# An encoder block on one core: the front is loaded in smaller pieces, and work is moved ahead of the plan

## The chip, the cores and the metric

The kernel runs on one core of a Trainium2 chip. The metric is the device time of one execution in microseconds, from the runs of one program; lower is better. TensorE (PE in the profile) does the matrix products, ScalarE (ACT) and VectorE (DVE) evaluate and split, GpSimd (POOL) takes a share of the elementwise work, and SyncE (SP) issues nearly all transfers.

## What is computed

One block of a hybrid encoder in float32 on 512 tokens of width 1024, with 16 learned meta tokens in front (528 columns). Two mixers work on the same normalized input: windowed attention with 16 query heads on 4 key heads, in a band of three 128-token blocks with the meta keys and a sink, and differential attention with 8 heads over all keys. Sigmoid gates merge them, and a gated feed-forward layer follows.

```python
u = rms_norm(h, pre_mix_gain[l])
proj = u @ w_in[l]
qa, ka, va, qb, kb, vb, g = jnp.split(proj, SPLITS, axis=-1)
...
o_swa = windowed_gqa_sink_attention(qa, ka, va, attn_sink[l], pos, is_real)
o_diff = differential_attention(qb, kb, vb, lam, lambda_init, subln_gain[l], is_key)
gates = jax.nn.sigmoid(g + b_gate[l])
merged = g_swa * (o_swa @ w_branch_swa[l]) + g_diff * (o_diff @ w_branch_diff[l])
h = h + rms_norm(merged @ w_out[l], post_mix_gain[l])
u = rms_norm(h, pre_ffn_gain[l])
f = (jax.nn.silu(gate_up[..., :D_FF]) * gate_up[..., D_FF:]) @ w_ffn_out[l]
```

## The kernel before

**Precision.** A float32 operand is split into a high part, rounded by a copy on ACT, and a low part, the difference, taken on DVE or POOL. Each product is made of three matmuls (`mm3`): high by high (L286), high weight by low input (L287), low weight by high input (L288). The third can't start before the whole low weight tile (`wl`) is written.

**Weights.** One tile of weights is 128 x 1024, 512 KB. SP loads it into one of three raw buffers (`wr`), ACT casts it (`wh`), DVE or POOL subtracts (`wl`). A raw buffer is free when the subtraction has read it, so a load in SP's queue can wait for POOL or DVE, and what stands behind it in the queue waits too. There are three slots each for `wh` and `wl`.

**The front** is written out by hand, L359 to L484, in the order in which each engine shall run it:

- 60 products of a zeroed tile (`warm`, L363) on PE.
- The input, transposed, comes in eight pieces `xr` of 264 KB (L375), and each is scaled by the gain on ACT (`xh`, L379), with its low part on DVE (`xl`, L380). Between them stand the weights of the two halves of the keys, in two pieces of 256 KB each (`w_half`, L388). All these transfers are issued by SP.
- The keys' products go through the eight input pieces k, twelve 264-column matmuls each, into `kA` and `kB`. Then the first value tile (`pV`, 48 matmuls, into the PSUM tiles `tr`).
- The sums of squares of the rows (`ss`, L440 and L442) give the row scale `rst`. Its columns are spread out on DVE (`rb`), transposed on PE (L454, L457), and copied by ACT to `rbc`. The keys' products are copied to `kraw`. `rbc` scales values (`VT`, L567), rotary factors (`rot`, L630) and all later evictions.

**The plan.** From there to the end of the differential attention (L621 to L1023), a table of tasks with costs, priorities and due times is scheduled by `Plan.run` while the program is built: each engine takes the task that is ready first and due first, at the plan's own costs. The result is a fixed order for each engine. Score products, transposes and products with the values have the first priority; the 512-column products of later weight tiles (queries, gates) are filler, put in wherever nothing more urgent is ready by the plan's clock. `held` takes over tiles made in the front.

The plan of before starts with the second value tile (`w3`) as a task. `v_swa` scales, transposes and splits the values. `rope_t` rotates keys and queries: products with `rot` on DVE (`ta`, `tb`, L533), a sum on POOL (L545), high part on ACT (L541) and low part on DVE (L537) into the one buffer `hl`. From there SP moves rows to the key tiles `KK` and query tiles `Q` (L555). `hl` holds the keys first; the queries' rotation writes it when the keys' moves have read it. `s_swa(u)` makes the scores of unit u of 16 (L692), `t_swa(u)` transposes them (L741) and multiplies by the values (L748). `gate(j)` is one gate tile of 24 matmuls of 512 columns. A table gives the unit after which each gate becomes available.

## Time and profile before

| | |
|---|---|
| time before, median of 3 runs | 983.13 us (981.66 to 983.18) |
| the profiled execution's own time | 984.33 us |
| its span, first to last instruction | 982.5 us |
| PE busy | 960.4 us, 98% |
| DVE, ACT, POOL busy | 572.5, 446.1, 287.8 us |

The span begins with the first instruction, and all times below count from there. The profiled execution is 1.83 us longer than its span, and 1.20 us above the median. The front fills about the first 26 us; the keys' and first queries' part of the plan lasts to 74 us, where the first scores stand; the windowed attention lasts to about 222 us. Behind 500 us PE has next to no idle time until its work ends.

### The profile page before, as it was taken

What the parts mean: (1) busy time and instruction counts of PE and PEld (TensorE: products, weight loads), DVE (VectorE), ACT (ScalarE), POOL (GpSimd) and SP (SyncE); (2) the same over time, 40 slices, a digit from 0 to 9 for tenths busy, and PEclk for the clock granted to TensorE, in tenths of its full rate; (3) what the DMA queues carried; (4) which work ended last, traced back from release to release, by engine and by line L of the source; (5) the groups of instructions that cost most, each with busy time, mean ns of one, the idle gap of its engine ahead of it and who ended that gap; (6) DMA issues with size and microseconds to landing.
All of it is one profiled execution on the core that took longest, in us unless ns stands there. A gap on an engine that the chain in (4) does not pass through costs nothing.

```text
span 982.5 us, 14257 instructions
## 1 busy us (share of the span) xinstructions
PE 960.4 (98%) x5307; PEld 825.3 (84%) x5307; DVE 572.5 (58%) x1061; ACT 446.1 (45%) x828; POOL 287.8 (29%) x262
## 2 busy tenths in 40 slices
PE   9899999999999999999999999999999999999997
PEld 9777777889798999999888888998888888888885
DVE  5836897899564758877765837843334333313224
ACT  6326676675634446667646434632222223222221
POOL 0543454453132423234203312653434300000000
PEclk9999999999999999999999999999999999999999
DMA  9482122251425144433531742343232323234122
GB/s 339 136 217 67 63 76 65 75 130 44 131 86 146 50 118 122 130 95 100 153 108 45 241 142 65 130 150 106 88 107 86 107 88 105 88 105 132 60 65 86
DMA packets 37141, 109.34 MB, mean 111 GB/s; under 512 B 6080, under 2 KB 6592, under 8 KB 37072
## 3 DMA queue, kind: packets, MB, share of 16 engines
q1 hardware_dynamic: 37072, 108.43, 36.4%
q8 instruction: 42, 0.69, 0.3%
q14 instruction: 27, 0.22, 0.1%
HBM read 87.04 MB, written 2.10 MB: 91 GB/s over the span
## 4 chain that ended last, share of the span: by engine, by line
PE 84%; DVE 8%; DMA 3%; issue 2%; SPq 2%; ACT 2%; DVEq 0%; POOL 0%; ACTq 0%
PE pr L287 18%; PE pr L288 18%; PE pr L286 18%; PE Sd L840 3%; PE Sw L692 2%; PE wk L288 2%; PE wk L286 2%; PE wk L287 2%; PE tr L288 2%; PE tr L287 2%; PE tr L286 2%; PE tr L880 2%; PE O L748 1%; PE Od L893 1%; PE acc L288 1%
## 5 line engine op out<-in xcount | busy, mean ns | idle before, releaser
L252 POOL TENSOR_TENSOR wl<-wr,wh 128x768 fp32r<-128x768 f32 (+1 forms) x76 | 170.8, 2248 | 235.0 <-ACT wh L271 155.7
L286 PE MATMUL pr<-xh,wh 128*128 128x264 f32 (+1 forms) x616 | 200.3, 325 | 0.0
L287 PE MATMUL pr<-xl,wh 128*128 128x264 f32 (+1 forms) x616 | 196.5, 319 | 0.4 <-DVE xl L380 0.4
L288 PE MATMUL pr<-xh,wl 128*128 128x264 f32 (+1 forms) x616 | 196.5, 319 | 0.3 <-POOL wl L252 0.3
L271 ACT CAST wh<-wr 128x1024 fp32r<-128x1024 f32 x78 | 81.9, 1052 | 216.5 <-PE pr L287 84.4
L252 DVE TENSOR_TENSOR wl<-wr,wh 128x1024 fp32r<-128x1024 f32 (+2 forms) x110 | 107.7, 980 | 121.0 <-ACT wh L271 109.1
L288 PEld LDWEIGHTS pr<-xh,wl 128*128 128x128 f32 x616 | 116.0, 188 | 9.0 <-POOL wl L252 0.5
L287 PEld LDWEIGHTS pr<-xl,wh 128*128 128x128 f32 x616 | 116.3, 189 | 8.1 <-DVE xl L380 0.6
L286 PEld LDWEIGHTS pr<-xh,wh 128*128 128x128 f32 x616 | 116.3, 189 | 7.4
L287 PE MATMUL pr<-ul,wh 128*128 128x512 f32 (+1 forms) x304 | 110.7, 364 | 0.3 <-DVE ul L252 0.3
L286 PE MATMUL pr<-uh,wh 128*128 128x512 f32 (+1 forms) x304 | 110.9, 365 | 0.0
L288 PE MATMUL pr<-uh,wl 128*128 128x512 f32 (+1 forms) x304 | 110.6, 364 | 0.0
L508 ACT CAST wh<-wr 128x1024 fp32r<-128x1024 f32 x56 | 58.6, 1049 | 43.7 <-PE pr L287 32.8
L287 PEld LDWEIGHTS pr<-ul,wh 128*128 128x128 f32 x304 | 57.4, 189 | 9.7 <-DVE ul L252 0.5
L288 PEld LDWEIGHTS pr<-uh,wl 128*128 128x128 f32 x304 | 57.3, 189 | 9.1
L286 PEld LDWEIGHTS pr<-uh,wh 128*128 128x128 f32 x304 | 57.3, 189 | 9.0
L545 POOL TENSOR_TENSOR ta<-ta,tb 128x528 f32<-128x528 f32 (+1 forms) x26 | 36.4, 1401 | 79.1 <-DVE tb L533 53.1
L845 DVE TENSOR_REDUCE nm<-Sd 128x1 f32<-128x528 f32 x64 | 45.2, 705 | 21.8 <-PE Sd L840 20.9
L308 POOL TENSOR_TENSOR r3y<-r3v,mhalf 128x1 f32<-128x1 f32 x4 | 2.2, 552 | 186.9 <-DVE r3v L307 186.9
L706 POOL TENSOR_SCALAR p<-p,rc 128x272 f32<-128x272 f32 (+1 forms) x64 | 37.1, 594 | 57.1 <-DVE rc L704 57.1
L848 ACT ACTIVATE pp<-Sd,nm 128x528 f32<-128x528 f32 x40 | 28.0, 700 | 39.3 <-DVE pa L861 22.6
L699 ACT ACTIVATE p<-p,nm 128x273 f32<-128x273 f32 (+1 forms) x64 | 36.7, 574 | 18.7 <-DVE nm L695 18.3
(377 smaller groups left out, 2000.4 us busy)
## 6 DMA issues: line engine op xcount, KB each, us to landing
wr<-in_w_in_dram SPq DMA_DIRECT2D x50, 512.0 KB, 4.2
wr<-in_w_fi_dram SPq DMA_DIRECT2D x50, 512.0 KB, 3.5
wr<-in_w_fo_dram SPq DMA_DIRECT2D x22, 512.0 KB, 3.5
Kd<-hl SPq DMA_DIRECT2D x32, 132.0 KB, 2.4
Kd<-Kd SPq DMA_DIRECT2D x16, 264.0 KB, 4.0
Q<-hl SPq DMA_DIRECT2D x64, 64.0 KB, 2.0
Qd<-hl SPq DMA_DIRECT2D x64, 64.0 KB, 2.5
wr<-in_w_bs_dram SPq DMA_DIRECT2D x8, 512.0 KB, 4.0
```

The source lines that it names most:

```text
L252: (eng or dve).tensor_tensor(out=lo, in0=src, in1=hi.bitcast(F32), op=ALU.subtract)
L271: act.copy(out=wh, in_=raw)
L286: pe.matmul(out=ps, lhsT=ah, rhs=bh, start=first, stop=False)
L287: pe.matmul(out=ps, lhsT=ah, rhs=bl, start=False, stop=False)
L288: pe.matmul(out=ps, lhsT=al, rhs=bh, start=False, stop=last)
L508: T("ACT", 1.05, lambda: act.copy(out=wh.t, in_=wr.t), r=[wr], w=[wh], prio=pr_)
L545: T("POOL", 0.05 + 1.3 * m, lambda: pool.tensor_tensor(out=ta.t[:, :, 0:n], in0=ta.t[:, :, 0:n], in1=tb.t[:, :, 0:n], op=ALU.add), r=[tb], ...
L699: T("ACT", 0.4 + 0.42 * c, lambda hh=hh: act.activation(out=pt.t[:, hh, 0:nk + 1], in_=pt.t[:, hh, 0:nk + 1], func=AF.Exp, scale=-1.0, bia ...
L706: T("POOL", 0.2 + 0.43 * c, lambda z=z: pool.tensor_scalar(out=pt.t[:, z, 0:nk], in0=pt.t[:, z, 0:nk], scalar1=rc.t[:, z:z + 1], scalar2=1 ...
L840: pe.matmul(out=S.t[:, s, 0:HALF], lhsT=Q[c].t[:, i * P:(i + 1) * P], rhs=K[c].t[:, x, s * HALF:(s + 1) * HALF], start=(x == 0), stop=(x = ...
L845: T("DVE", 0.71, lambda S=S, c=c, one=one: dve.tensor_reduce(out=nm.t[:, c, one], in_=S.t[:, :, 0:HALF], axis=AX.XY, op=ALU.min), r=[S], w ...
L848: T("ACT", 0.9, lambda S=S, c=c, one=one, p=p: act.activation(out=p().rearrange("p (a b) -> p a b", a=2), in_=S.t[:, :, 0:HALF], func=AF.E ...
```

## The change

- The keys' weights come in three pieces, k 0, k 1 to 3 and k 4 to 7 (64, 192 and 256 KB). ACT issues the first piece of both halves and the second piece of the first half; SP issues the rest. The split of a piece is called apart from its load.
- 40 zero products instead of 60.
- The second value tile is multiplied in the front, half of it ahead of the transposes of the row scale and half behind. `kraw` is copied ahead of the sums of squares.
- The first query tile's weights are loaded and split in the front, the low part on POOL.
- The plan starts with engines free at other times (`free`), slots and SP at earlier ones, and two tables are changed: gates 2 to 5 become available after units 1, 8, 11, 14 instead of 0, 1, 2, 8, and the first two counts of `b1` are swapped.

```diff
@@ Plan @@
-        self.slots = {t: [0.0] * n for t, n in tags.items()}
+        self.slots = {t: [-9.0] * n for t, n in tags.items()}
...
-        free = dict.fromkeys(("PE", "ACT", "DVE", "POOL", "SP"), 0.0)
-        port = 0.0
+        free = dict(PE=0.0, ACT=-1.2, DVE=-1.2, POOL=-0.5, SP=-3.0)
+        port = -9.0
...
-                    t = 0.0
+                    t = -9.0
@@ front @@
-    for _ in range(60):
+    for _ in range(40):
         pe.matmul(out=wps[:, 0:P], lhsT=warm, rhs=warm, start=True, stop=True)
...
-    def w_half(w, n, h):
-        if h == 0:
+    def w_part(w, n, k0, k1, eng):
+        if k0 == 0:
             w.extend([...])
-        ks = slice(h * KT // 2, (h + 1) * KT // 2)
-        sp.dma_start(out=w[0][:, ks], in_=I["w_in"][n].rearrange("p (k c) -> p k c", k=KT)[:, ks])
-        split(w[1][:, ks], w[2][:, ks], w[0][:, ks])
+        ks = slice(k0, k1)
+        eng.dma_start(out=w[0][:, ks], in_=I["w_in"][n].rearrange("p (k c) -> p k c", k=KT)[:, ks])
+        return lambda: split(w[1][:, ks], w[2][:, ks], w[0][:, ks])
...
     x_load(0)
-    w_half(wA, 0, 0)
+    sa = w_part(wA, 0, 0, 1, act)
+    sb_ = w_part(wB, 1, 0, 1, act)
+    x_load(1)
+    sa1 = w_part(wA, 0, 1, 4, act)
+    sa()
     x_split(0)
-    w_half(wB, 1, 0)
-    for k in range(1, KT):
+    sb1 = w_part(wB, 1, 1, 4, sp)
+    sb_()
+    x_load(2)
+    x_split(1)
+    sa1()
+    sb1()
+    for k in range(3, KT):
         x_load(k)
-        x_split(k)
-        if k == 2:
-            w_half(wA, 0, 1)
-            w_half(wB, 1, 1)
+        x_split(k - 1)
+        if k == 3:
+            sa2, sb2 = (w_part(w, n, 4, KT, sp) for n, w in enumerate((wA, wB)))
+        if k == 4:
+            sa2()
+            sb2()
+    x_split(KT - 1)
...
     for h in range(2):
         proj(pV[h], wV, X, h * HALF, (h + 1) * HALF)
+    kraw = [...]
+    for s in range(2):
+        cs = slice(s * HALF, (s + 1) * HALF)
+        act.copy(out=kraw[0][:, cs], in_=kA[s])
+        act.copy(out=kraw[1][:, cs], in_=kB[s])
+    pV2 = [pr_t(HALF), pr_t(HALF)]
+    proj(pV2[0], wV2, X, 0, HALF)
...
     pe.transpose(out=Sw[:, 1, 0:P], in_=rb, identity=ident)
+    proj(pV2[1], wV2, X, HALF, EXT)
     act.copy(out=rbc[:, NMETA:EXT], in_=rps)
     act.copy(out=rbc[:, 0:NMETA], in_=Sw[:, 1, 0:NMETA])
+    wQ = [...]
+    sp.dma_start(out=wQ[0], in_=I["w_in"][4].rearrange("p (k c) -> p k c", k=KT))
+    act.copy(out=wQ[1], in_=wQ[0])
+    sub_hi(wQ[2], wQ[0], wQ[1], pool)
@@ plan @@
-    w3 = [pl.held(t, x) for t, x in zip(("wh", "wl"), wV2)]
+    WQ = [pl.held(t, x) for t, x in zip(("wh", "wl"), wQ[1:])]
...
-        wa, wb = weights(I["w_in"][4 + 2 * g], dep), weights(I["w_in"][5 + 2 * g], dep)
+        wa, wb = weights(I["w_in"][4 + 2 * g], dep) if g else WQ, weights(I["w_in"][5 + 2 * g], dep)
...
-    v_swa([products(w3, X, X_, h * HALF, (h + 1) * HALF) for h in range(2)])
+    v_swa(PV2)
...
-        for j in {0: (2,), 1: (3,), 2: (4,), 8: (5,)}.get(u, ()):
+        for j in {1: (2,), 8: (3,), 11: (4,), 14: (5,)}.get(u, ()):
...
-        for _ in range((4, 3, 0, 1, 0, 0, 0, 0)[h]):
+        for _ in range((3, 4, 0, 1, 0, 0, 0, 0)[h]):
```

Because the plan is made anew, instructions move on every engine. Three places matter below. The first is ACT from its first instruction to the first inputs. Before:

```order
L621 ACT_TABLE_LOAD
L621 CAST aTm<-zero 128x256 x2
L256 CAST wh<-wr 128x512
L379 ACTIVATE xh<-xr,vec 128x528
L256 CAST wh<-wr 128x512
L379 ACTIVATE xh<-xr,vec 128x528 x2
L256 CAST wh<-wr 128x512 x2
```

The same place now (lines count in the changed text):

```order
L388 DMA wr<-in_w_in_dram 128x128 x2
L388 DMA wr<-in_w_in_dram 128x384
L256 ACT_TABLE_LOAD
L256 CAST wh<-wr 128x128
L643 CAST aTm<-zero 128x256 x2
L379 ACTIVATE xh<-xr,vec 128x528
L256 CAST wh<-wr 128x128
L379 ACTIVATE xh<-xr,vec 128x528
L256 CAST wh<-wr 128x384 x2
L379 ACTIVATE xh<-xr,vec 128x528 x2
```

Three issues stand ahead of the table load, and the casts of `aTm`, which the front doesn't need, stand between the first weights and the first input.

The second is POOL from the power of the row scale (`r0y`) to the third weight tile; `vr` are value columns for the meta keys, `ta` the sums of the rotation. Before:

```order
L308 TENSOR_TENSOR r0y<-r0v,mhalf 128x5
L683 COPY p<-nsink 128x4 x2
L575 COPY vr<-VT 128x128
L252 TENSOR_TENSOR wl<-wr,wh 128x1024
L480 CAST bdm<-zero 128x256 x2
L545 TENSOR_TENSOR ta<-ta,tb 128x528 x2
L575 COPY vr<-VT 128x128
```

And now:

```order
L308 TENSOR_TENSOR r0y<-r0v,mhalf 128x5
L705 COPY p<-nsink 128x4 x2
L252 TENSOR_TENSOR wl<-wr,wh 128x1024
L502 CAST bdm<-zero 128x256 x2
L252 TENSOR_TENSOR wl<-wr,wh 128x1024
L597 COPY vr<-VT 128x128
L567 TENSOR_TENSOR ta<-ta,tb 128x528 x2
L597 COPY vr<-VT 128x128
```

POOL now subtracts both tiles of the first queries ahead of the first `vr` and of the keys' sums; before, it had one of them and DVE the other.

The third is DVE where the keys' rotation ends (the second `hl` of 264 columns) and that of the first queries begins (`ta` and `tb` out of `pr`, the queries' products). `ta` out of `pr` needs the first query tile's 24 products, `tb` those of the second too. Before:

```order
L252 TENSOR_TENSOR wl<-wr,wh 128x1024
L252 TENSOR_TENSOR Vs<-tr,Vs 128x8x64
L606 SCALAR_TENSOR_TENSOR Vm<-tr,vec,Vm 128x2x64
L537 SCALAR_TENSOR_TENSOR hl<-ta,hl 128x2x16
L533 TENSOR_TENSOR ta<-pr,rot 128x2x256
L537 SCALAR_TENSOR_TENSOR hl<-ta,hl 128x2x264
```

And now:

```order
L252 TENSOR_TENSOR Vs<-tr,Vs 128x8x64
L628 SCALAR_TENSOR_TENSOR Vm<-tr,vec,Vm 128x2x64
L555 TENSOR_TENSOR tb<-pr,rot 128x2x256
L559 SCALAR_TENSOR_TENSOR hl<-ta,hl 128x2x16
L555 TENSOR_TENSOR ta<-pr,rot 128x2x256
L559 SCALAR_TENSOR_TENSOR hl<-ta,hl 128x2x264
```

The keys' last `hl` was behind `ta` of the queries; it is now behind `tb`, so behind the products of the second query tile. On PE, 153 matmuls of 512 columns stood ahead of the first scores and 177 stand there now, one gate tile more; between the first scores and those of the differential attention there are 24 fewer of them, and 15 more of 264 columns.

More of the change, by code (lines that the diff above doesn't have):

```diff
@@ L137, in held @@
         b.tile = tile
-        b.slot = self.slots[tag].index(0.0)
+        b.slot = self.slots[tag].index(-9.0)
         self.slots[tag][b.slot] = None
@@ L431, in encoder @@
         proj(pV[h], wV, X, h * HALF, (h + 1) * HALF)
+    kraw = [atp.tile([P, EXT], F32, tag="q", name="kraw", bufs=8) for _ in range(2)]
+    for s in range(2):
[4 more added lines that the diff above has]
+    proj(pV2[0], wV2, X, 0, HALF)
     ss = const.tile([P, 5], F32, name="ss")
@@ L443, in encoder @@
                                      op0=ALU.mult, op1=ALU.add, accum_out=ss[:n, t:t + 1])
-    kraw = [atp.tile([P, EXT], F32, tag="q", name="kraw", bufs=8) for _ in range(2)]
-    for s in range(2):
-        cs = slice(s * HALF, (s + 1) * HALF)
-        act.copy(out=kraw[0][:, cs], in_=kA[s])
-        act.copy(out=kraw[1][:, cs], in_=kB[s])
     rst = rsqrt_cols(const, ss, P, 1.0 / D, "r0")
@@ L457, in encoder @@
     pe.transpose(out=Sw[:, 1, 0:P], in_=rb, identity=ident)
+    proj(pV2[1], wV2, X, HALF, EXT)
     act.copy(out=rbc[:, NMETA:EXT], in_=rps)
     act.copy(out=rbc[:, 0:NMETA], in_=Sw[:, 1, 0:NMETA])
+    wQ = [wp.tile([P, KT, P], d, tag=t, name=t, bufs=n) for t, d, n in (("wr", F32, RB), ("wh", F32R, 3), ("wl", F32R, 3))]
+    sp.dma_start(out=wQ[0], in_=I["w_in"][4].rearrange("p (k c) -> p k c", k=KT))
+    act.copy(out=wQ[1], in_=wQ[0])
+    sub_hi(wQ[2], wQ[0], wQ[1], pool)
     pool.tensor_scalar(out=hb, in0=vec[:, 8:24], scalar1=0.5, scalar2=1.0, op0=ALU.mult, op1=ALU.mult)
@@ L624, in encoder @@
     MK = [pl.held("rt", t) for t in (mk1, mk2)]
-    PV = [pl.held("tr", t) for t in pV]
+    PV, PV2 = [pl.held("tr", t) for t in pV], [pl.held("pr", t) for t in pV2]
     for b in MK:
```

## The prediction

> **What bounds the kernel now.** I read the page's busy times and chain first, then a table by stretches of the span, then PE's waits, then the timelines of the front.
>
> ```profile
> PE 960.4 (98%) x5307; PEld 825.3 (84%) x5307; DVE 572.5 (58%) x1061; ACT 446.1 (45%) x828; POOL 287.8 (29%) x262
> PE 84%; DVE 8%; DMA 3%; issue 2%; SPq 2%; ACT 2%; DVEq 0%; POOL 0%; ACTq 0%
> ```
>
> PE bounds it: 960.4 of 982.5 us. The change removes 20 zero products and no other PE work, so it can only shift the start of that work and the holes in it. Where are they?
>
> ```profile
> 25.00:30.00 5.00, 4.34 (x33) 3.77 (x32) 3.77 (x12) 2.80 (x6) 2.44 (x5) 1.00 0.57 190
> 30.00:40.00 10.00, 7.70 (x50) 6.42 (x49) 9.97 (x16) 3.28 (x7) 7.18 (x7) 1.00 0.17 55
> ...
> 100.00:150.00 50.00, 48.25 (x245) 38.22 (x244) 43.30 (x119) 33.43 (x86) 23.49 (x36) 1.00 0.23 71
> 150.00:200.00 50.00, 48.31 (x284) 40.68 (x284) 40.95 (x112) 33.71 (x86) 26.46 (x38) 1.00 0.21 57
> 200.00:250.00 50.00, 47.78 (x339) 43.63 (x338) 44.84 (x103) 32.47 (x76) 20.49 (x24) 1.00 0.37 94
> ...
> 800.00:900.00 100.00, 100.00 (x443) 82.79 (x442) 32.07 (x32) 27.08 (x32) 0.00 (x0) 1.00 0.34 110
> ```
>
> The columns are the stretch, its length, then busy time and count of PE, PEld, DVE, ACT, POOL, and clock, DMA share, GB/s. The front (25 to 40) loses 3.0 us. The windowed attention loses 1.7 to 2.2 per 50 us, with DVE 82 to 90% busy: PE and DVE are nearly level there. The last row gives the pitch of a 512-column matmul, 100/443 = 0.226 us. What ends the front's holes:
>
> ```profile
> PE tr L585 <- DVE VT L567: 2.3, 2, 1.6
> ...
> PE rps L454 <- PE tr L288: 0.6, 1, 0.6
> PE pr L287 <- DVE xl L380: 0.4, 1, 0.4
> ```
>
> and behind them the wait for the first queries' moves, below. The wait put down to PE itself ends with DVE's `rb`, which the next fence shows.
>
> **The change part by part.** The start:
>
> ```profile
> 0.97 6.06 PE L363 MATMUL wps<-warm 128*128 128x128 bf16 x60 [0.97 <-DVE warm L360]
> ...
> 7.05 0.31 PE L287 MATMUL pr<-xl,wh 128*128 128x264 f32 x1
> ...
> 9.29 0.39 PE L287 MATMUL pr<-xl,wh 128*128 128x264 f32 x1 [0.41 <-DVE xl L380]
> ...
> 19.43 0.28 PE L286 MATMUL tr<-xh,wV 128*128 128x264 f32 x1
> ...
> 25.15 0.28 PE L288 MATMUL tr<-xh,wV 128*128 128x264 f32 x1
> 26.08 0.69 PE L454 MATMUL rps<-ident,rb 128*128 128x128 f32 x4 [0.65 <-PE tr L288]
> ...
> 26.72 0.37 PE L286 MATMUL pr<-xh,wh 128*128 128x264 f32 x1
> ```
>
> 48 matmuls from 19.43 to 25.15 are 47 steps of 0.122 us: an input piece (12) costs 1.46, a value half (24) 2.92.
>
> ```profile
> 0.72 1.28 ACT L621 ACT_TABLE_LOAD   x1 [0.72 <-PEq L1292]
> 2.01 0.71 ACT L621 CAST aTm<-zero 128x256 fp32r<-128x256 f32 x2
> ...
> 5.38 0.73 ACT L379 ACTIVATE xh<-xr,vec 128x528 fp32r<-128x528 f32 x1
> ```
>
> ```profile
> 6.15 0.77 DVE L380 SCALAR_TENSOR_TENSOR xl<-xr,vec,xh 128x528 fp32r<-128x528 f32 x1
> 6.83 0.68 DVE L252 TENSOR_TENSOR wl<-wr,wh 128x512 fp32r<-128x512 f32 x1
> ...
> 25.75 0.63 DVE L453 COPY rb<-r0y 128x128 f32<-128x128 f32 x4
> ```
>
> ```profile
> 1.64 0.91 SPq L388 DMA_DIRECT2D wr<-in_w_in_dram  x2
> ```
>
> The first pair of products can run when `xl` of piece 0 is there. ACT now issues three transfers first. No row shows an issue on ACT; SP's are 0.46 each, so three end at 2.1 (bounds: 0.7 if they cost ACT nothing, 3.5 if twice SP's). Then the table 1.28, a cast of 128 columns (0.3, between the 0.18 of 16 and the 0.59 of 512 in the rows of `rbc` below), `aTm` 0.71 and `xh` 0.73: 5.1, then `xl` 0.77: 5.9, against 7.05. The 40 zero products end near 0.97 + 40 x 0.107 = 5.2, the pitch by 20 in a window of 2 us below, so they don't hold PE. From there DVE sets the pace up to piece 4: five `xl` of 0.77 and weights worth 2 x 0.2, 2 x 0.5 and 2 x 0.68, 6.6 us from 5.1, so the `xl` of piece 4 is there at 11.7 if no transfer is late, and PE at 1.46 a piece comes to it at 5.9 + 4 x 1.46 = 11.7 too. The values then start at 17.5; with late pieces (piece 1 kept PE until 9.29 before) or the dearer issues up to 18.9. I take 17.9, nearer the first end because the pieces ahead of input piece 1 shrink by 384 KB: **gain 1.5** (0.5 to 1.9).
>
> The value half in front of the transposes starts at 17.9 + 5.8 = 23.7 and ends at 26.7, behind `rb` of 25.75 (set by the last rows of x, a transfer that isn't moved). It covers the hole of 25.27 to 26.08: **gain 0.8** (0.5 to 0.8). Its cover is 0.9 us; were `rb` later by more than that, the rest comes back. `kraw` ahead of the squares costs nothing as long as the last rows of x, not ACT, end the squares; without that cover it delays `rb`, which has these 0.9 to spare.
>
> Now the first query's weights.
>
> ```profile
> 25.68 1.05 ACT L508 CAST wh<-wr 128x1024 fp32r<-128x1024 f32 x1 [0.98 <-DMA wr<-in_w_in_dram]
> 26.80 0.59 ACT L458 COPY rbc<-rps 128x512 f32<-128x512 f32 x1
> 27.29 0.18 ACT L459 COPY rbc<-Sw 128x16 f32<-128x16 f32 x1
> ```
>
> ```profile
> 28.24 4.00 POOL L252 TENSOR_TENSOR wl<-wr,wh 128x1024 fp32r<-128x1024 f32 x1
> ...
> 50.34 2.41 POOL L252 TENSOR_TENSOR wl<-wr,wh 128x1024 fp32r<-128x1024 f32 x1
> ```
>
> ```profile
> 28.19 1.80 DVE L630 TENSOR_TENSOR rot<-rot,rbc 128x1584 f32<-128x1584 f32 x1
> 29.90 2.42 DVE L471 CUSTOM_DVE_ANT_0 lj<-lt 128x64 f32<-128x64 f32 x1
> ...
> 32.26 0.41 DVE L471 CUSTOM_DVE_ANT_0 lj<-lt 128x64 f32<-128x64 f32 x1
> ```
>
> Before, this cast stood ahead of `rbc`; now it stands behind both copies, which end 0.75 behind the transposes. PE: transposes done at 26.7 + 0.6 = 27.3, second value half until 30.2, two query products, 30.7, then L288 needs `wl`. ACT: `rbc` at 28.1, cast until 29.1, and POOL takes 2.41 alone or 4.00 beside `rot`: 31.5 to 33.1. `rot` starts 0.3 after `rbc` plus one eviction now, so it overlaps POOL by about 1.0 instead of 1.75; I take 3.4: 32.6. **A new stall, loss 1.9** (0.8 to 2.4); before, 48 value products covered this tile. A gain is excluded: PE had no wait here.
>
> The two waits for `VT` (2.3): the first is covered, since 12 query products now stand ahead of its transposes. The second `VT` of the second tile stands behind `lj`, three rotations, the mean of lambda and the split of the first values. `lj` ended when POOL's subtraction did (29.90 + 2.42 = 32.3), so I let two of the rotations wait for POOL's second subtraction, which now follows at once: DVE is done near 40.5, PE arrives near 39.5. Loss 1.0 left (0 to 2.3), **gain 1.3**. The Trainium skill, page "SBUF — State Buffer", section "Who interferes with whom", states that a DVE instruction with two inputs in SBUF and a GpSimd instruction that reads SBUF exclude each other for a whole instruction; the 2.42 against 0.41 agrees. Without that rule the rotations would pass, nothing would be left of the wait, and the sum would be better by 1.0.
>
> The first scores:
>
> ```profile
> 44.13 0.71 DVE L537 SCALAR_TENSOR_TENSOR hl<-ta,hl 128x528 fp32r<-128x528 f32 x1 [0.46 <-ACT hl L541]
> ...
> 48.25 0.69 DVE L533 TENSOR_TENSOR tb<-pr,rot 128x512 f32<-128x512 f32 x1 [1.55 <-PE pr L288]
> ```
>
> ```profile
> 74.42 1.09 PE L692 MATMUL Sw<-KK,Q 128*128 128x272 f32 x4 [1.87 <-DMA Q<-hl]
> ```
>
> Keys' `hl` done (44.84), their moves, then the queries' `hl` and moves, landed at 74.42: 29.6 us. Now the keys' last `hl` waits for `tb`, so for the second query tile's products. Call their end T (48.2 before). `tb`, the small `hl`, `ta`, `hl` are 0.69 + 0.15 + 0.69 + 0.71 = 2.2, so Q lands at T + 31.8. PE had 24.3 from T to its wait; with 24 more products (5.4) it arrives at T + 29.7. The hole is 2.1 instead of 1.87: **loss 0.3**. In SP's queue a weight load now stands between the keys' moves, for a slot that DVE frees two operations later, up to 3 more; if the moves are quicker, the hole closes, up to 1.9 gained. So -3.3 to +1.9.
>
> The other edits have no instructions of their own: plan times, gate table and `b1` counts only set the order. Of the windowed attention 24 products of 0.226 go ahead, and 15 of 0.122 come in: 3.6 us less filler. At a PE-bound stage this costs nothing, being only moved.
>
> Sum: 1.5 + 0.8 - 1.9 + 1.3 - 0.3 = 1.4 us. The profiled execution took 984.33, 1.83 of it outside the span; it would take 982.9. The median of before is 983.13, so **981.7**.
>
> **Rivals.**
>
> ```profile
> 1.00:3.00 2.00, 2.00 (x20) 1.00 0.43 80
> ...
> 6.30:6.90 0.60, 0.60 (x12) 1.00 0.93 303
> ```
>
> ```profile
> 72.55:74.42 1.87, 0.00 (x0) 0.03 (x1) 0.00 (x0) 0.00 (x0) 1.26 (x1) 1.00 0.52 121
> 74.60:78.00 3.40, 3.40 (x12) 2.79 (x12) 1.08 (x5) 1.12 (x4) 0.00 (x0) 0.50 0.45 154
> ```
>
> *The clock isn't up in time* (0.12). The zero products run at half pitch until about 6.3 and at full pitch behind it, though the clock column says 1.00 throughout; and a hole of 1.87 is followed by 3.4 us at a granted clock of 0.50. Now PE pauses from 5.2 to 5.9, but for one product. If that keeps it slow for another 3.4 us, half of 3.4 is lost, 1.7, a little of it behind late inputs: gain 1.4 falls to 0, 983.1. Against it: the pause is a third of the hole that did trip it. The Trainium skill, "TensorE: Matmul & The Clock Gate", section "What's actually happening", says that the full clock comes after a busy window of about 3.4 us that runs freely; 40 products of 0.107 us fill such a window for certain only in some phases. The row at 6.3 agrees with one such window; the phase of other executions no row shows.
>
> *The scores' chain paces the stage* (0.18, the slower side). From the first score to the last, scores, softmax, transposes and values follow each other over DVE at 82 to 90%. If that chain and not PE sets the stage's length, the first score's time decides: at 74.42 before, and at 74.42 + 5.4 - 1.4 = 78.4 now, 4.0 later; the 15 narrow products done inside give back 1.8. With SP's load in the way by half of its 3 us, 3.7 is lost: 986.8, and without it 985.3; call it 985.9. For it: DVE's share, and 24 fewer products of cover. Against: PE is 96% busy there. It decides once the moved filler exceeds what PE wants.
>
> *The hole at the scores closes* (0.25). If SP's queue runs the moves quicker, the 2.1 goes, and with it the half clock, up to 1.7: 1.4 + 2.1 + half of 1.7, 978.8. For it: 24 more products stand ahead of the scores, and the 29.6 us hold 0.71 of rotation and for the rest mostly transfers behind one another. Against: the chain starts 5.5 later.
>
> **How the numbers follow.** The forecast has 0.45, 981.7 with an own range of 980 to 983.3. This kernel's measurement tells about 0.2% (2.0 us) from no change: faster lies below 981.2, slower above 985.1. Faster: 0.19 of the forecast and 0.24 of the closed hole, 0.43. Slower: most of the chain rival, 0.16. Within: 0.41. The range of 8 in 10 takes in the closed hole and the milder chain: 978.2 to 985.3.
>
> **What would show it.** First pair of products near 5.9 and values at 17.9; no wait ahead of `rps`; PE waiting for POOL's `wl` for about 1.9 near 31; one wait for `VT` instead of two; a wait for Q of about 2 at 77, the half clock behind it; the windowed attention shorter by about 3.6. I am wrong if PE does not wait for `wl`, if the stage keeps its length, or if holes behind 100 us change by over 2 us: those I took as unchanged.

## The result, and the profile after

The change made the kernel slower: 989.53 us median (989.03 to 990.53), beside 983.15 us of the kernel before on the same chip. The ratio is 1.0069, with an interval of 1.0052 to 1.0087. The forecast was 981.7 us, with a range up to 985.3. All times are medians of executions in the fast state; only jit_land had others, two of its eleven (1179 and 1920 us), and they are left out.

The page of the changed kernel, its span and busy times (the profiled execution took 990.53 us):

```profile
span 988.7 us, 14224 instructions
PE 959.4 (97%) x5287; PEld 821.7 (83%) x5287; DVE 582.4 (59%) x1062; ACT 446.2 (45%) x830; POOL 294.1 (30%) x263
```

PE works 1.0 us less than before (960.4); its zero products alone take 1.6 us less (4.45 for 6.06). The span is 6.2 us longer. So PE has 7.2 us more of idle time. DVE is busy 9.9 us longer (572.5 before), with one instruction more.

Where is the idle time? I cut both executions at the same places of the program: the first score product (`Sw`), the first score product of the differential attention (`Sd`), the first product of the merging weights, the last product. Columns as in the prediction's table of stretches: the stretch, its length, then busy time and count of PE, PEld, DVE, ACT, POOL, then clock, DMA share, GB/s. Before:

```profile
0.00:74.42 74.42, 68.20 (x420) 59.55 (x421) 42.66 (x67) 32.00 (x50) 27.48 (x33) 1.00 0.73 228
74.42:217.37 142.95, 136.92 (x744) 111.98 (x745) 118.28 (x323) 96.36 (x242) 66.59 (x103) 0.99 0.30 82
217.37:522.98 305.61, 302.93 (x2001) 273.62 (x2000) 216.06 (x407) 173.99 (x336) 89.51 (x68) 1.00 0.37 105
522.98:976.00 453.02, 452.30 (x2145) 380.13 (x2143) 192.28 (x258) 143.38 (x202) 103.70 (x58) 1.00 0.33 105
```

And after:

```profile
0.00:78.56 78.56, 72.23 (x424) 62.05 (x425) 44.36 (x70) 34.15 (x54) 30.85 (x34) 1.00 0.72 223
78.56:216.94 138.38, 131.51 (x732) 108.18 (x732) 116.71 (x321) 94.62 (x239) 67.82 (x102) 1.00 0.29 81
216.94:528.28 311.34, 302.96 (x1991) 271.37 (x1990) 224.82 (x407) 173.09 (x335) 91.60 (x70) 1.00 0.37 103
528.28:982.00 453.72, 452.65 (x2145) 380.13 (x2143) 193.01 (x257) 143.63 (x202) 103.31 (x58) 1.00 0.33 105
```

Length less PE's busy time is PE's idle time: 6.22, 6.03, 2.68 and 0.72 us before; 6.33, 6.87, 8.38 and 1.07 us after. The first two rows are the part that the prediction worked out. The changed kernel comes to the first differential score 0.43 us sooner, and has done 12 recorded products more by then (424 + 732 less 40 zero ones against 420 + 744 less 60). At 0.122 to 0.226 us a product that is a lead of 1.9 to 3.1 us. **The third row loses that lead and more**: 5.7 us of additional idle time, at the same PE work (302.93 and 302.96 us). There DVE needs 8.8 us more for the same 407 instructions.

PE's waits after, over the whole span (engine, line, what it waited for: us in total, times, longest):

```profile
PE Sw L714 <- DVE nm L717: 6.1, 12, 1.5
PE Sd L862 <- ACT pp L870: 1.9, 3, 1.1
PE pr L288 <- POOL wl L252: 1.7, 1, 1.7
PE pr L286 <- DVE tb L555: 1.6, 1, 1.6
PE Od L907 <- ACT aTm L906: 1.4, 1, 1.4
PE mp L930 <- DVE sl L252: 1.3, 1, 1.3
PE pr L286 <- DVE VT L589: 1.3, 1, 1.3
PE tr L902 <- DVE pp L883: 1.2, 1, 1.2
...
PE Sw L714 <- DMA Q<-hl: 0.4, 1, 0.4
```

The waits for `wl`, `tb`, `VT` and `Q` lie in the front. Those for `aTm`, `sl` and the two for `pp` belong to the differential attention (`pp` are a head's softmax weights, `aTm` transposed ones for the meta keys, `sl` the low part of squares); before, none of the kind was longer than 0.7 us. Two stretches of the differential attention hold nearly all of it, its second head and its last one up to the merging. Before, then after:

```profile
260.61:316.60 55.99, 55.99 (x338) 49.80 (x339) 33.23 (x57) 27.55 (x47) 15.47 (x10) 1.00 0.36 104
442.88:522.98 80.10, 80.10 (x445) 67.75 (x444) 53.39 (x97) 49.96 (x91) 20.17 (x15) 1.00 0.38 113
```

```profile
261.72:307.40 45.68, 42.92 (x278) 38.47 (x279) 31.29 (x51) 24.92 (x44) 13.44 (x9) 1.00 0.34 94
445.46:528.28 82.82, 79.40 (x428) 65.45 (x427) 57.53 (x97) 49.37 (x90) 22.03 (x15) 1.00 0.36 109
```

PE had no idle time in either, and now has 2.76 and 3.42 us. Both stretches hold fewer products than before (278 for 338, 428 for 445). In the first, 60 of the 120 512-column filler products have moved elsewhere, so the softmax of a head is less covered; in the second it is only 18 of 264 columns. Something else shows in the timelines of DVE and POOL (start, duration); the first two lines are from the second head, the others from the last stretch:

```profile
272.08 2.95 DVE L945 SCALAR_TENSOR_TENSOR ob<-ob,g,y 128x512 f32<-128x512 f32 x1
...
288.87 2.11 DVE L880 TENSOR_TENSOR rc<-rc,nlam 128x1 f32<-128x1 f32 x1
...
450.98 2.71 DVE L945 SCALAR_TENSOR_TENSOR ob<-ob,g,y 128x512 f32<-128x512 f32 x1
...
522.26 2.15 DVE L252 TENSOR_TENSOR sl<-sq,sh 128x512 fp32r<-128x512 f32 x1
```

```profile
272.10 2.39 POOL L252 TENSOR_TENSOR wl<-wr,wh 128x1024 fp32r<-128x1024 f32 x1
...
288.57 2.38 POOL L252 TENSOR_TENSOR wl<-wr,wh 128x1024 fp32r<-128x1024 f32 x1
...
450.76 2.38 POOL L252 TENSOR_TENSOR wl<-wr,wh 128x1024 fp32r<-128x1024 f32 x1 [1.37 <-ACT wh L530]
...
521.84 2.02 POOL L252 TENSOR_TENSOR wl<-wr,wh 128x768 fp32r<-128x768 f32 x1 [14.85 <-ACT wh L271]
```

A DVE instruction of 512 columns takes about 0.7 us (the experiment on the collision, below, shows `sl` at 0.68), the one of a single column, `rc`, 0.16 us. Beside a POOL subtraction the long ones ended about half a microsecond after POOL's end, `rc` right at it. DVE runs from each of the four without a pause to what PE then waits for: `pp` (1.07 us) by way of `nm`, a reduction of the scores, `pp` (1.19), `aTm` (1.38) and `sl` itself (1.28). Each wait is shorter than what the DVE instruction lost (2.2, 1.9, 2.0 and 1.5 us). So 4.9 of the 8.4 us of idle time in the third row stand directly behind such collisions.

The same can be counted in all traces. I call a DVE instruction of the differential attention held up if it took over 0.15 us longer than the faster quarter of its kind. Before, 7 are, by 5.1 us in all; in the changed kernel 15 are, by 14.5 us. Each of them overlaps a POOL instruction, in every one of the eighteen traces. The difference of 9.5 us covers the 8.8 us that DVE needs more.

### The profile page after: what moved, and what is told of

The parts are those of the page before. It is cut to its first block, busy times and chain, and to the rows that moved or that the text cites. A ratio compares the mean times of both kernels' runs of the same rounds, so it can differ in the third digit from the quotient of the medians.

```text
span 988.7 us, 14224 instructions
## 1 busy us (share of the span) xinstructions
PE 959.4 (97%) x5287; PEld 821.7 (83%) x5287; DVE 582.4 (59%) x1062; ACT 446.2 (45%) x830; POOL 294.1 (30%) x263
## 5 line engine op out<-in xcount | busy, mean ns | idle before, releaser
L252 POOL TENSOR_TENSOR wl<-wr,wh 128x768 fp32r<-128x768 f32 (+2 forms) x77 | 171.6, 2229 | 240.6 <-ACT wh L271 152.9
L252 DVE TENSOR_TENSOR wl<-wr,wh 128x1024 fp32r<-128x1024 f32 (+4 forms) x111 | 108.4, 978 | 117.9 <-ACT wh L271 109.9
L862 PE MATMUL Sd<-Kd,Qd 128*128 128x264 f32 x256 | 43.2, 291 | 2.6 <-ACT pp L870 1.9
```

The lines of the kernel that those rows point to most:

```text
L252: (eng or dve).tensor_tensor(out=lo, in0=src, in1=hi.bitcast(F32), op=ALU.subtract)
L862: pe.matmul(out=S.t[:, s, 0:HALF], lhsT=Q[c].t[:, i * P:(i + 1) * P], rhs=K[c].t[:, x, s * HALF:(s + 1) * HALF], start=(x == 0), stop=(x = ...
```

## The experiments

Two theories stood at first: that the front itself costs (new stalls, the clock), or that the front gains about what was forecast, and the order made anew by the plan loses more. Later questions were why an order loses, and why a gain at the first products doesn't reach the end. The table has all kernels that ran; ratios are to the kernel before on the same chip, whose median was 982.2 to 983.15 us. "Differential" is the stretch of the third row above, cut in the same way. It and the first score come from one profiled execution each.

| kernel | order behind the front | ratio to before | first score, us | differential: PE idle, DVE busy, us |
|---|---|---|---|---|
| before | its own | 1 | 74.42 | 2.68, 216.06 |
| start_only | before's | 1.0012 [1.0001, 1.0023] | 73.90 | 3.63, 216.23 |
| kept_order | before's, replayed | 1.0024 [1.0013, 1.0035] | 75.83 | 3.18, 216.16 |
| kept_order60 | before's, replayed | 1.0014 [1.0004, 1.0024] | 75.15 | 2.77, 216.21 |
| lambda_early | before's | 0.9971 [0.9960, 0.9981] | 72.56 | 2.05, 216.19 |
| lambda_start | before's | 0.9977 [0.9968, 0.9987] | 72.36 | 2.13, 216.16 |
| rows_start | before's | 0.9968 [0.9956, 0.9980] | 71.02 | 2.58, 216.18 |
| jitter_before | before's (nothing moved) | 1.0003 [0.9994, 1.0012] | 74.45 | 1.94, 216.09 |
| jit_land | made anew | 1.0025 [1.0016, 1.0035] | 74.37 | 5.00, 218.61 |
| after | made anew | 1.0069 [1.0052, 1.0087] | 78.56 | 8.38, 224.82 |
| after_again | the same | 1.0079 [1.0067, 1.0092] | 77.51 | 8.74, 224.89 |
| no_coll | the same | 1.0077 [1.0064, 1.0091] | 79.61 | 8.30, 224.22 |
| new_tables | made anew | 1.0132 [1.0103, 1.0161] | 74.23 | 8.74, 223.32 |
| jit_after | made anew | 1.0158 [1.0143, 1.0174] | 77.55 | 13.21, 233.00 |
| parity_old | made anew | 1.0169 [1.0155, 1.0183] | 76.16 | 14.42, 222.96 |
| jit_act | made anew | 1.0202 [1.0183, 1.0220] | 74.49 | 13.14, 222.80 |
| same_parity | made anew | 1.0221 [1.0203, 1.0238] | 76.14 | 11.07, 224.06 |
| old_gates | made anew | 1.0289 [1.0273, 1.0306] | 79.65 | 18.61, 232.90 |

### Which part of the change costs

**start_only**: the kernel before with the keys' loads in pieces and 40 zero products, nothing else. Its plan, and so the order behind the front, stays.

```diff
-    for _ in range(60):
+    for _ in range(40):
-    w_half(...)
+    w_part(...)   # the change's lines from x_load(0) to the last x_split
```

> Only the start of the changed kernel in the kernel before: keys' weights in three pieces from two queues, 40 zero products. The plan and its order stay as before. The milestones of both profiles put the values 1.27 us earlier in the changed kernel (18.16 against 19.43). Theory 'the front's gain is real and the plan made anew loses it': 1.0 to 1.5 us faster than before, since behind the values the order is the same; but the row scale waits for the last rows of x (rb at 25.75 in the profile before), so part of it may end in the hole ahead of rps: then 0 to 0.5 us. Rival 'the front itself does harm later, by its timing': slower than before.

983.18 us (980.62 to 985.24), 1.0012 [1.0001, 1.0023]: no gain, and a loss of 0.1% that is just clear of the interval. Its values started at 19.61, no sooner than before. The timeline of PE shows why; first and last rows of a stretch of products that follow each other at 0.22 us, and then at 0.12:

```profile
5.69 0.59 PE L286 MATMUL pr<-xh,wh 128*128 128x264 f32 x1 [0.27 <-ACT xh L379]
...
6.88 0.42 PE L288 MATMUL pr<-xh,wl 128*128 128x264 f32 x1
7.10 0.42 PE L286 MATMUL pr<-xh,wh 128*128 128x264 f32 x1
...
9.94 0.29 PE L287 MATMUL pr<-xl,wh 128*128 128x264 f32 x1
10.07 0.28 PE L288 MATMUL pr<-xh,wl 128*128 128x264 f32 x1
```

The products run at half pace until 9.9, where the changed kernel's profile has 0.12 from 6.3. This is the rival "the clock isn't up in time", seen in this execution. Over the nine profiled executions with 40 zero products it happened in three (start_only, old_gates and no_coll, with the values at 19.6 to 20.0), and in six not (values at 17.7 to 18.2). In the nine with 60 zero products it didn't happen (full pitch by 7.3 at the latest; in the three of them with the smaller pieces the values are at 18.0 to 18.4).

**same_parity**: the change, with the plan's counter of weight tiles starting at 1. An odd count gives a tile's subtraction to POOL, an even one to DVE. The change takes the first query tile out of the count, so all later tiles swap engines; this undoes the swap.

```diff
-    nfill = [0]
+    nfill = [1]
```

> The changed kernel with its count of weight tiles starting at 1, so that each later tile's low part is subtracted by the same engine as in the kernel before (in the change the first query tile isn't counted, so POOL's and DVE's tiles swap through the whole plan). Theory 'parity' (the swap makes POOL and DVE collide at the wrong places): most of the 6.4 us comes back, 981 to 984. Theory 'tables' (gates available later): no effect, 988 to 991. Theory 'any plan made anew': somewhere between 981 and 992, with other holes.

1002.92 us, 1.0221. Undoing a side effect cost another 14 us (20.7 above the kernel before on the same chip, where the change has 6.4).

**old_gates**: the change with the gate table of before.

```diff
-        for j in {1: (2,), 8: (3,), 11: (4,), 14: (5,)}.get(u, ()):
+        for j in {0: (2,), 1: (3,), 2: (4,), 8: (5,)}.get(u, ()):
```

> The changed kernel with the gate table of before (units 0, 1, 2, 8 instead of 1, 8, 11, 14), the b1 counts stay as changed. Theory 'tables': the filler is back early, the loss between units 9 and 11 goes, 981 to 985. Theory 'parity': no effect, 988 to 991. Theory 'any plan made anew': between 981 and 992, with other holes.

1010.16 us, 1.0289. **new_tables**: the kernel before with the change's gate table and `b1` counts, and nothing else of it.

```diff
-        for j in {0: (2,), 1: (3,), 2: (4,), 8: (5,)}.get(u, ()):
+        for j in {1: (2,), 8: (3,), 11: (4,), 14: (5,)}.get(u, ()):
...
-        for _ in range((4, 3, 0, 1, 0, 0, 0, 0)[h]):
+        for _ in range((3, 4, 0, 1, 0, 0, 0, 0)[h]):
```

> The kernel before with the gate table and the b1 counts of the change, nothing else. Theory 'tables': 3 to 8 us slower than before, 986 to 991, with holes between units 9 and 11. Theory 'parity': no change, 982 to 984. Theory 'any plan made anew': anything from 981 to 991.

994.21 us, 1.0132. So the two new tables lose 12 us with the old front, while the new gate table is better than the old by some 21 us with the new front. No edit has a price of its own: each re-made order has one. (The `b1` counts alone were not tried.)

### The order alone

**kept_order**: the front of the change, and the tasks behind it in the order of the kernel before, written out as a list and replayed. Gate table, `b1` counts and the counter's parity are those of before, so that both have the same tasks. **parity_old** has exactly these tasks, but the plan orders them anew.

```diff
     def run(self):
-        (the plan's search for the next task of each engine)
+        for n in ORDER:        # the order of the kernel before
+            ... issue task n
```

> The front of the changed kernel as it is (pieces, 40 zero products, second value tile, first query tile ahead of the plan), but behind it each engine's order is word for word that of the kernel before: the order is replayed from a list instead of being made anew, with the tables and the assignment of tiles to POOL and DVE of before. Theory 'the front gains, the order made anew loses': the front's gain stays, 1.3 to 3.5 us by the milestones (values 1.27 us earlier, the lost time at the scores of unit 8 lower by 3.5), so 979 to 982. Rival 'the front itself does harm later (first scores and DVE, POOL in other phases)': 984 to 990, as the changed kernel.

> The same tasks as kept_order (front of the change, tables and assignment of tiles of before), but the order is made anew by the changed plan. It differs from kept_order in the order alone. Theory 'order made anew': 5 to 25 us slower than kept_order, 985 to 1005. Rival 'tables and assignment are what matters': like kept_order, within 2 us.

985.38 us (1.0024) and 999.44 us (1.0169). **The same front and the same tasks differ by 14 us by their order alone.** (With the order goes the choice among equal buffers.) So an order can cost that much. The change's own order and tables cost less: 1.0069 for 1.0024 with the same front, about 4.4 us. And with the order kept, the front doesn't gain: 985.38 lies in the range of the rival, in which the front itself does harm, and 2.8 us above the kernel before. **kept_order60** has 60 zero products, in case the clock took it away:

> As kept_order, with 60 zero products again. Theory 'the clock rises in whole windows of 3.4 us, and the gap behind 40 products can lose one' (seen where PE stayed at half clock until 9.90 and 10.36 instead of 6.15): the first products start about 1 us later than with 40, but the clock is up by 7.5 in every execution, so the spread of the times shrinks and the median is the same or up to 0.8 us lower. Rival 'the gap is harmless': 0.7 to 1.2 us slower than kept_order, by the later start.

983.45 us, 1.0014 [1.0004, 1.0024]: no gain over the kernel before either. The values start at 18.0 to 18.1, 1.4 us sooner than before, and the first score comes later, at 75.15 and 75.83.

**jitter_before** was meant to disturb the plan of the kernel before and see how much its order matters.

```diff
+        free["ACT"] = 0.3
```

> The kernel before, with one number of the plan changed: ACT is taken to be free 0.3 us later at the plan's start. No work is changed, only the order that the plan makes of it. Theory 'any plan made anew': it lands 3 to 25 us away from 983, likely above. Rival 'the plan is robust, and the change's tables or front are at fault': within 1 us of 983.

982.73 us, 1.0003. This run tells nothing of that: the edit didn't move one instruction, so it is the kernel before a second time. What it gives is the spread: 0.03% between the two, with an interval of 0.9994 to 1.0012.

### How much an order is worth

So the disturbance was made again, with costs that do move it. **jit_land** and **jit_act** are the kernel before, **jit_after** the changed kernel:

```diff
-          w=[wr], dep=dep, prio=pr_, land=3.6 if nfill[0] > 3 else 0.3)
+          w=[wr], dep=dep, prio=pr_, land=3.8 if nfill[0] > 3 else 0.3)     # jit_land
-        T("ACT", 1.05, lambda: act.copy(out=wh.t, in_=wr.t), ...)
+        T("ACT", 1.06, lambda: act.copy(out=wh.t, in_=wr.t), ...)           # jit_act, jit_after
```

> The kernel before, with one cost that only the plan reads changed: a weight's load takes 3.8 instead of 3.6 us. It moves 19 pieces of PE's order and 23 of VectorE's, and no task is added or taken. Theory (a re-made order is worth several us either way by chance, and the kernel before holds a lucky one): over 2 us away from the kernel before, slower rather than faster, 0 to 12 us. Rival (the plan is robust, and what the re-made orders lost is due to the change's own edits, parity and gates): within 1 us, ratio 0.999 to 1.001.

> The kernel before, with one cost that only the plan reads changed: a weight's cast takes 1.06 instead of 1.05 us. It moves 74 pieces of PE's order and 124 of VectorE's, and no task is added or taken. Theory (re-made orders differ by chance): over 2 us away from the kernel before, slower rather than faster, 0 to 15 us. Rival (the plan is robust): within 1 us.

> The changed kernel, with one cost that only the plan reads changed: a weight's cast takes 1.06 instead of 1.05 us, which moves 79 pieces of PE's order and adds no task. Theory (the changed kernel's 6.4 us are one draw from orders that differ by chance): over 2 us away from 989.5, on either side, between 984 and 1005. Rival (the 6.4 us belong to the change's own edits): 988.5 to 990.5.

984.50 us (1.0025), **1001.87 us (1.0202)** and 998.84 us (1.0158). A cost that only the plan reads, changed by 0.01 us, is worth 19 us to the kernel before and 8 to the changed one (998.84 beside 990.60 on the same chip). In jit_act the table by stretches has this row for the differential attention:

```profile
223.21:543.77 320.56, 307.42 (x1993) 276.55 (x1992) 222.80 (x406) 175.62 (x339) 88.70 (x67) 0.98 0.35 98
```

13.1 us of idle time, and 4.5 us more of busy time at nearly the same products (the clock column says 0.98). The wait that grew most is the scores' for the softmax, first of PE's waits:

```profile
PE Sd L840 <- ACT pp L848: 8.5, 6, 2.9
```

Eight orders were made anew with one edit or another, and all eight were slower than the order of the kernel before, by 0.25 to 2.9%. The last column of the table goes along with it: DVE needs 216.1 to 216.2 us wherever the order is kept, and 218.6 to 233.0 us for 405 to 409 instructions where it isn't. By the count above, DVE loses 5.0 to 5.2 us to POOL in the kept orders and 6.7 to 20.9 us in the re-made ones, so in the order of the kernel before the two meet less. The idle time doesn't simply follow that count: jit_act has fewer collisions than the changed kernel (10.5 us) and more idle time (13.1). In five of the eight a part of the loss lies ahead of this stage: its first score comes at 222.3 to 229.6 us (new_tables, parity_old, jit_act, same_parity, old_gates), for 217.4 before.

### One collision

**no_coll**: the changed kernel with the first weight tile behind the plan subtracted on DVE alone, so that `sl` (2.15 us in the fence above) has no POOL instruction beside it.

```diff
-        cut = 3 * k // 4 if 4 <= nw[0] < 52 else 0
+        cut = 3 * k // 4 if 5 <= nw[0] < 52 else 0
```

> The changed kernel, with the first weight tile behind the plan split on VectorE alone instead of three quarters on GpSimd; nothing else moves on any engine. In the changed kernel GpSimd's wl<-wr,wh of 128x768 ran at 521.84 to 523.86, and VectorE's sl<-sq,sh of 128x512 beside it took 2.15 us instead of 0.69. Theory (the two engines shut each other out while both read two operands from SBUF): sl takes 0.7 us, PE's wait of 1.3 us for sl goes, end 0.8 to 1.3 us sooner than the changed kernel: ratio to before 1.0056 to 1.0061 where the changed kernel has 1.0069. Rival (sl is late for another reason): sl stays at 2 us and the time is the changed kernel's within 0.4 us.

> The changed kernel itself beside the other three of this call, for their differences: 989 to 990.5 us.

DVE's timeline in no_coll:

```profile
522.91 1.22 DVE L252 TENSOR_TENSOR wl<-wr,wh 128x1024 fp32r<-128x1024 f32 x1 [0.16 <-ACT wh L271]
524.05 0.68 DVE L252 TENSOR_TENSOR sl<-sq,sh 128x512 fp32r<-128x512 f32 x1
```

`sl` takes 0.68 us, and PE's wait for it falls from 1.28 to 0.44. So POOL made it slow. In the time it can't be seen: 990.19 us (988.61 to 992.34) beside 990.60 us (989.08 to 991.50) of the changed kernel on the same chip. The idle time of the stage is 8.30 us, where two executions of the changed kernel have 8.38 and 8.74: one wait of the scores for the transfer of a weight tile, 1.6 us here and 0.5 and 1.3 there, takes part of the 0.8 us back. The other collisions were not taken away; that they cost PE what stands behind them is read from the trace.

### Why the front's gain doesn't reach the end with the order kept

With the order kept, the time from the first score to PE's last product hardly depends on the front: 900.8 us before, 900.6 in start_only, 900.5 and 899.8 in the kept orders. (jitter_before, the same program as before, has 898.9, so this time varies by about 2 us between executions.) So the first score is what the front can move, and PE waits for it. The theory is that a chain sets it: the last rows of x, `rb`, `rps`, `rbc`, `rot`, the keys' rotation, the moves of keys and queries. DVE's `lj` (two sums for lambda) stands in that chain before; it took 2.42 us beside POOL. **lambda_early** takes it out:

```diff
+    qt = atp.tile([P, EXT], F32, tag="q", name="qt", bufs=8)
+    lt = qt[:, 0:256]...; lj = qt[:, 256:384]...
+    sp.dma_start(out=lt, in_=I["lam"])
     sp.dma_start(out=ident, in_=I["ident"])
...
     dve.tensor_copy(out=rb, in_=rst[:, 4:5].broadcast_to([P, P]))
+    (the two sums of lambda)
...
-    (load of lambda and the two sums)
```

> The kernel before, with lambda's two small sums (lj<-lt on VectorE, 2.42 and 0.41 us in the profile before, between rot and the keys' rotation) moved into VectorE's idle 0.98 us ahead of rbc, and their load ahead of ident's. The plan and all orders behind it stay. Theory (the chain last rows of x, rbc, rot, keys' rotation, moves sets the first score, PE only waits for it): the wait for Q (1.9 us) goes, the first score starts at 72.5 to 73.2 instead of 74.42, and since the same order takes 900.5 us from there, the end comes 1.2 to 1.9 us sooner: ratio about 0.9985. Rival 1 (the move of Q is limited by the products before it, not by the keys' chain): first score stays at 74 and ratio 1.000. Rival 2 (what is gained at the first score is lost behind it): first score earlier, ratio 1.000.

979.79 us, **0.9971 [0.9960, 0.9981]**. DVE's timeline has the sums ahead of `rbc`, and PE's timeline the first score:

```profile
26.55 0.22 DVE L463 CUSTOM_DVE_ANT_0 qt<-qt 128x64 f32<-128x64 f32 x1
...
26.70 0.41 DVE L463 CUSTOM_DVE_ANT_0 qt<-qt 128x64 f32<-128x64 f32 x1
```

```profile
72.56 0.73 PE L693 MATMUL Sw<-KK,Q 128*128 128x272 f32 x4 [1.02 <-DMA Q<-hl]
```

The first score is 1.86 us sooner, and the products before it started no sooner than in the kernel before (7.05 for 6.84). The chain sets it. What comes after takes 898.9 us to the last product, no more than in jitter_before. **lambda_start** adds the change's pieces (the diff of start_only, but for the zero products, which stay 60):

> lambda_early, with the change's loads of the keys' weights in pieces from two queues, and 60 zero products; order behind as before. Theory: products start at 5.7 to 6.0, the values at 17.9, rps at 25.5 as in the first-part-only kernel, and with the keys' chain short PE arrives at the first score at about 72.0: the end 2.0 to 2.5 us sooner than before, ratio about 0.9976, so 0.5 us more than with lambda alone. Rival (the gain of the front never passes rps, which waits for the rows of x): ratio as that of lambda_early.

980.07 us, 0.9977. The rival came true: the values start at 18.43, but the first score at 72.36 is only 0.2 us sooner than in lambda_early. PE stands 1.25 us ahead of `rps`, which needs the rows of x. **rows_start** loads these ahead of the second value tile's weights:

```diff
+    (loads of the rows of x and of the meta rows)
     wV2: load
-    (loads of the rows of x and of the meta rows)
...
-    wV2: cast and subtraction
+    (cast behind the squares; subtraction on DVE behind the copies to rb;
+     lambda's sums while DVE waits for the power of the row scale)
```

> lambda_start (keys' weights in pieces, 60 zero products, lambda's sums out of the keys' chain), with the rows of x and the meta rows loaded ahead of the second value tile's weights instead of behind them (2.06 MB, at some 400 GB/s of the profile 5.2 us; the tile's 0.5 MB take 1.3 us); lambda's sums between r0h and r0z; the second value tile's low parts (1.23 us) behind the rb copies. Theory (what the front gains doesn't pass rps, because the rows land at 22.1; the chain rows, rbc, rot, moves sets the first score): rps at 24.3 to 24.6 instead of 25.68, PE waits up to 0.7 us for the low parts behind it, first score at 71.1 to 71.8 instead of 72.36, end 0.6 to 1.3 us sooner than lambda_start. Rival (PE's own work sets the first score once Q's wait is gone, or the later start of the second value tile costs what rps gains): within 0.4 us of lambda_start or later.

```profile
23.97 0.69 PE L483 MATMUL rps<-ident,rb 128*128 128x128 f32 x4
...
25.60 0.39 PE L288 MATMUL pr<-xh,wl 128*128 128x264 f32 x1 [0.50 <-DVE wl L252]
...
71.02 0.73 PE L715 MATMUL Sw<-KK,Q 128*128 128x272 f32 x4 [0.19 <-DMA Q<-hl]
```

`rps` is 1.7 us sooner, the first score 1.34, a little more than the theory had, and of the wait for Q 0.19 us is left. The time is 979.26 us, 0.9968 [0.9956, 0.9980]: faster than before, but against lambda_start's 0.9977 [0.9968, 0.9987] the two intervals overlap, so whether the 1.3 us reach the end is open. lambda_early and rows_start beat both kernels, by 0.3% and 1.0 to 1.1%.

## Why the prediction was wrong

**Up to the first differential score the steps came out.** Forecast and then measured in the changed kernel:

- *The start*, gain 1.5, values at 17.9: they start at 18.16, a gain of 1.27. ACT's three issues took 1.38 us, 0.46 each, as SP's do. The first `xl` is there at 6.1 instead of 5.9. The zero products end at 5.42 instead of 5.2 (the row that the prediction names gives 0.100 us a product, not its 0.107); they hold PE in neither case.
- *The value half ahead of the transposes*: no wait ahead of `rps`, which starts at 26.94 (forecast 26.7).
- *The stall for POOL's `wl`*, 1.9: 1.66. POOL's subtraction took 3.38 us (forecast 3.4) and ended at 32.64 (32.6).
- *`VT`*, 1.0 left: one wait of 1.27 us.
- *The wait for Q*, 2.1 at 77 with half the clock behind it: the keys' last `hl` is done at 48.68 and Q lands at 78.56, 29.9 us later (29.6 forecast). PE waits only 0.44 there, but it waited 1.56 us for `tb` at 63. The two make 2.0. The half clock didn't come: the column says 1.00, and the longest hole was 1.66 us, where 1.87 before was followed by half the clock.
- *The first score* at 78.4: 78.56. *The windowed attention shorter by 3.6*: 138.38 instead of 142.95, by 4.6. The rival in which the scores' chain paces this stage falls with that, and so does the closed hole.

The lead at the first differential score, 1.9 to 3.1 us, is no less than the forecast gain of 1.4.

**The step that failed** is the paragraph "The other edits have no instructions of their own: plan times, gate table and `b1` counts only set the order", with its price of nothing, and with it the holes behind 100 us ("those I took as unchanged"). The order behind the front costs 5.7 us of additional idle time in the differential attention, a stage that the prediction didn't cost at all. PE was busy there for 302.93 of 305.61 us before, and the prediction's "PE bounds it" took a nearly full PE as given. It was full because the order was a good one. The runs show it in three ways: the same tasks in the old order are 14 us faster than in a new one; a 0.01 us tweak costs 19 us; and all eight re-made orders were slower. The prediction said what would make it wrong, "if holes behind 100 us change by over 2 us", but gave that no chance among its rivals.

What the idle time consists of is settled in part. In the changed kernel's trace, 4.9 us of PE's waits in that stage stand directly behind four DVE instructions that POOL held up. One of these collisions was taken away, and the wait behind it fell by 0.8 us; the other three are read from the trace alone. With more products to cover them they need not have cost anything, so cover has a part too, and how much is open: jit_after has as many products as the changed kernel in that stage (1991) and 4.8 us more idle time, so the number of covering products isn't all. Nor are collisions in other orders, as jit_act shows. The plan keeps such instructions of DVE and POOL apart by its own clock (`port` in the diff); on the chip they meet all the same.

**A second point that the result hides**: the front's forecast gain of 1.4 us belongs to the changed order, not to the front. With the order of before it isn't there: kept_order and kept_order60 are slower than before by 0.1 to 0.2%. There the first score hangs on the rows of x and the keys' chain, and the start's products are not on it, as lambda_early, lambda_start and rows_start show with the value half at its old place. In the kept orders PE takes the value half first, and `rps` comes at 26.8, 0.7 us later than before, and the first score 1.4 and 0.7 us later. The prediction priced the value half with a gain of 0.8 and this delay of `rps` with nothing. In the changed order the chain begins at PE's own products, T, as the prediction had it, and there a late start passes on: in no_coll the half pitch lasted until 10.35, the values came 1.6 us later than in after_again (19.71 for 18.08), the first score 2.1 us later, and the span is 1.7 us longer (989.0 for 987.3).

*The rival on the clock* was rightly described, and not the cause here: the changed kernel's two profiles have the full pitch from 6.3 at the latest. It happens in some executions with 40 zero products (three of nine) and not in others.

## What to carry to other kernels

Where a planner sets the order, an edit that it sees can draw a new order. Before costing such an edit, disturb the planner by a cost that changes nothing else and time a few orders: that spread (here 0.25 to 2.9%, all to one side, since the order in use was the best of them) is the price, and an edit worth 1 us can't be judged without keeping the order fixed. And ask of a gain which chain ends at the next point where engines meet: here, with the order kept, 1.7 us at the first values was worth 0.2 us at the first score (lambda_start beside lambda_early), and moving two tiny VectorE instructions out of the keys' chain was worth 0.3%.

## What the runs showed of the hardware

- **VectorE and GpSimd shut each other out.** `ob` took 2.71 us and `sl` 2.15 beside POOL, `sl` 0.68 without; `lj` took 2.42 us in the kernel before and 0.22 in lambda_early. POOL's `wl` in turn took 3.38 and 4.00 us beside `rot`, 2.38 beside `ob`, which it held up. The additional DVE time of the re-made orders (up to 17 us in the differential attention, 233.00 in jit_after against 216.06) is nearly all in instructions that overlap one of POOL's (20.9 us held up in jit_after, 5.1 before); that each would be quick without POOL was shown for `sl` and `lj` alone. The Trainium skill, "SBUF — State Buffer", section "Who interferes with whom", says that a DVE instruction with two inputs in SBUF contends with a GpSimd instruction that reads SBUF, and that the contended ports are an exclusive lock; the ends of these instructions agree, as `ob` ended 0.55 us after POOL's, and so does no_coll.
- **The clock can fall or stay down for part-time work.** In kept_order, PE waited for `VT` twice, 2.4 us from 34.1 and 1.4 us from 37.0. Half the clock was granted for 6.7 us from 34.7 on, and PE was busy for half of them:

```profile
34.70:41.40 6.70, 3.45 (x10) 2.70 (x11) 6.67 (x11) 2.28 (x4) 5.01 (x4) 0.50 0.15 58
```

- **With 40 warm-up products the half pitch sometimes lasted until about 10 us.** In start_only PE stood still for 0.27 and 0.22 us between the first products and kept the half pitch until 9.9; the changed kernel, with 0.22 us of such a wait, was at full pitch from 6.3. The length of the pause doesn't decide it: no_coll had the same 0.22 us and kept the half pitch until 10.35, and after_again had 0.24 and 0.42 us and was at full pitch from 6.2. The clock column says 1.00 for all of them, and only the steps between products show it. The Trainium skill, "TensorE: Matmul & The Clock Gate", section "What's actually happening", has windows of about 3.4 us that run freely; the 3.6 us from 6.3 to 9.9 agree with one window missed. That this is the cause, no run here shows.
